# Memory keys of a decoder step: two column groups multiplied in turn, staggered first transfers, squares spread over later units

## The chip, the core and the metric

The kernel runs on one core of a Trainium2 chip, launched once. The metric is the device time of the launch in microseconds, the median of three runs. TensorE (PE) multiplies, ScalarE (ACT) and VectorE (DVE) work on rows of 128 partitions, GpSimd (POOL) and SyncE (SP) issue transfers, and every engine works through its own queue of instructions in the order in which they were placed there; semaphores hold an instruction until what it reads is there or what it overwrites has been read.

## The reference, cut to what matters

One layer of a decoder: an input projection, three branches (sliding-window attention, a state-space branch, attention into 256 memory tokens), a merge and a feed-forward block, for 256 prompt tokens and 8 samples. The change lies in the first part, which computes keys and values of the memory tokens:

```
def _rmsnorm(x, g):
    y = x * lax.rsqrt(jnp.mean(jnp.square(x), axis=-1, keepdims=True) + EPS)
    return y * g

def _mem_kv(mem, norm_mem, w_mem_kv, k_norm_mem):      # mem (256, 2048), w_mem_kv (2048, 2048)
    b, m, _ = mem.shape
    k, v = jnp.split(_rmsnorm(mem, norm_mem) @ w_mem_kv, 2, axis=-1)
    k = _rmsnorm(k.reshape(b, m, MEM_HEADS, MEM_HEAD_DIM), k_norm_mem)
    return k, v.reshape(b, m, MEM_HEADS, MEM_HEAD_DIM)
```

The rest follows on one core and is not touched; it reads the memory keys and values late.

## The kernel before, in words

**Units.** All weights are worked through as a list of units. A unit is a tile `raw` of 128x1024 fp32 (two blocks of 128 rows by 512 columns, 512 KB), loaded by SP (L261), split by ACT into a rounded part `hi` (L181) and by DVE into the remainder `lo` (L182), and multiplied on PE (L160). There are four `raw` buffers and three of `hi` and `lo`; `feed(i)` issues the load of unit i+4 and the split up to unit i+2 ahead of the products of unit i. A new `hi` waits until the last product of the unit three in front has read its buffer.

**Memory part.** Units 0 to 31. The product has 256 rows (two tiles of 128 memory tokens, `t`) and 2048 columns in four groups of 512: groups 0 and 1 are the keys, 2 and 3 the values. Each group is eight units, one after the other, and accumulates in two PSUM tiles `pmem` of 128x512. A unit gives 12 products of 128x512: two row blocks, two token tiles, and three terms each (`hi`x`memh`, `lo`x`memh`, `hi`x`meml`). `memh` and `meml` are the features: the rows of `mem_prompt`, loaded in pieces by `load_mem` (tiles `ring` for the first 128 tokens, `mem` for the second), transposed on PE (`memT`, L164) and split by ACT (`memh`, L348) and DVE (`meml`, L349) in `mem_feats`. The features of unit u+1 of group 0 are issued behind the first products of unit u.

**PSUM.** Two pools fill it: five tiles of 128x512 that the accumulators and the warm-up tile `idle` share, and three for short uses (`memT`, `kmT`, `rbx`, ...). A tile goes to a new user when the last reader of its old one is done.

**Norms.** `mem_norm` sums squares of the rows (eight ACT instructions of 128x512, `junk`, L360), then DVE forms `msv` and, by a shift and three Newton rounds (L171 to L176), `rs_m`. After the last unit of a key group `after_k` runs: four ACT sums `jk` (L404) that need `rs_m`, a chain of short DVE instructions, `km` (L413), its transposes `kmT` on PE and their copies on ACT. Values are scaled and stored by `after_v`. `prep_x` does for the rows of x what comes ahead of the input projection: sums of squares (`jkx`, L472), the inverse root, its spread `dgx`, `rbx`, then transposes `xT`.

**Order.** A scheduler sets each engine's queue from the order in the program, by its own estimates of time; `tc.issue_after(x)` holds what follows behind x. `mem_norm` and `prep_x` are generators that hand out a piece after each unit once they are ready (`rows` at unit 1, `go` at unit 9).

Of the kernel before, what the change touches and what calls it, by code (L numbers as in the profile page):

```python
# [23 lines left out]
KT = D // P  # L24
# [53 lines left out]
def tile_hybrid_decoder_step(  # L78
# [118 lines left out]

    def load_mem(f, n):

        for t in range(2):  # L200
            queue = nc.scalar if t and f < 2 else nc.sync
            h = f // 4
            if (t, h) not in mem_t:
                mem_t[t, h] = (lm if t else ld)("mem")
            c = slice(256 * (f % 4), 256 * (f % 4 + n))
            d = queue.dma_start(mem_t[t, h][:, c], mem_prompt[0, t * P:(t + 1) * P, h * 1024:(h + 1) * 1024][:, c])
            if f == 1:
                first["load1"] = d
# [48 lines left out]
    def load():  # L257
        n = state["dma"]
        raw = wp.tile([P, 1024], F32, tag="raw", name=nm("raw"), bufs=4)
        for j, (sl, src) in enumerate(units[n]["loads"](raw)):  # L260
            d = (nc.scalar if n == 0 and j else nc.sync).dma_start(sl, src)  # L261
        for f in behind.get(n, ()):
            with tc.issue_after(d.ins):
                f()
        raws[n] = raw
        state["dma"] += 1

    def feed(i):
        while state["dma"] < min(i + N_DMA + 1, len(units)):
            n = state["dma"]  # L270
            load()
            while state["split"] <= n - (N_DMA - N_SPLIT):
                do_split(state["split"])
        while state["split"] < min(i + N_SPLIT, len(units)):
            do_split(state["split"])

    def do_split(n):
# [12 lines left out]
        else:  # L290
            for k in range(2 if n == 0 else 1):
                c = slice(512 * k, 512 * k + 512) if n == 0 else slice(0, 1024)
                with tc.issue_after(state["memh", k if n == 0 else 1].ins):
                    state["split_at"], state["rest_at"] = split(hi[:, c], lo[:, c], raw[:, c])
# [57 lines left out]
    def mem_norm():  # L352
        junk = t2("junk", BF16)[:, 0:512]
        ssm_ = tiny("ssm", 8)
        for h in range(2):
            for t in range(2):
                for c in range(2):
                    o = 4 * t + 2 * h + c
                    with tc.issue_after(state["split_at"].ins):
                        act(junk, mem_t[t, h][:, c * 512:(c + 1) * 512], AF.Square, accum_out=ssm_[:, o:o + 1])  # L360
                    yield 0.6
        turn_vectors()
# [5 lines left out]
        yield 2  # L368

    def mem_group(cg):  # L370
        st = {}

        def prod(u):
            def f(hi, lo):
                if u == 0:
                    st["ps"] = [dps("pmem") for _ in range(2)]
                for n, (t, k) in enumerate(((0, 0), (1, 0), (0, 1), (1, 1))):
                    if cg == 0 and n == 1 and u < 7:

                        with tc.issue_after(m.ins):  # L380
                            mem_feats(u + 1)
# [4 lines left out]
                    mm(st["ps"][t], mh, wh, start=kk == 0, stop=False)  # L386
                    mm(st["ps"][t], mh, wl, start=False, stop=False)
                    m = mm(st["ps"][t], ml, wh, start=False, stop=kk == KT - 1)
# [36 lines left out]
        def loads(u):  # L425
            std = std_loads(w_mem_kv[0, 2 * u * P:(2 * u + 2) * P, cg * 512:(cg + 1) * 512])

            def f(raw):
                if cg == 0 and u in (1, 2, 4, 6):
                    load_mem(u, 1 if u == 1 else 2)  # L430
# [6 lines left out]
        for u in range(KT // 2):  # L437
            units.append(dict(
                loads=loads(u), 
                prod=prod(u), after=(after_k if cg < 2 else after_v) if u == KT // 2 - 1 else None))  # L440

    for cg in range(4):
        mem_group(cg)
# [1250 lines left out]
    side.add("m", mem_norm(), ["rows"])  # L1694
# [17 lines left out]
    load()  # L1712
    load()
# [5 lines left out]
    with tc.issue_after(state["turn"].ins):  # L1719
        warm_up(4)  # L1720
    for i, u in enumerate(units):
        feed(i)
        if i == 1:
            side.ready.add("rows")
        if i == 7:
            side.drain("m")
        if i == 9:
            side.ready.add("go")
# [45 lines left out]
```

## Time and profile before

| | |
|---|---|
| three runs | 1918.14, 1921.36, 1923.82 us; median 1921.36 |
| profiled execution | 1919.56 us, of which the span of the trace is 1917.8 us |
| PE busy | 1896.4 us, 99% of the span, 15359 matmuls |
| DVE, ACT, POOL busy | 1175.2, 961.2, 115.6 us |
| memory part | the first 90 us or so of the span |

The profile is of one execution on the one core. Times are counted from the start of the span. Busy time of a matmul runs to its modelled end, and matmuls overlap, so the distance from start to start tells what a product costs on the engine. A bracket behind a row tells how long the engine stood idle ahead of it and what ended that.

### The profile page before, as it was taken

What the parts mean: (1) busy time and instruction counts of PE and PEld (TensorE: products, weight loads), DVE (VectorE), ACT (ScalarE), POOL (GpSimd) and SP (SyncE); (2) the same over time, 40 slices, a digit from 0 to 9 for tenths busy, and PEclk for the clock granted to TensorE, in tenths of its full rate; (3) what the DMA queues carried; (4) which work ended last, traced back from release to release, by engine and by line L of the source; (5) the groups of instructions that cost most, each with busy time, mean ns of one, the idle gap of its engine ahead of it and who ended that gap; (6) DMA issues with size and microseconds to landing.
All of it is one profiled execution on the core that took longest, in us unless ns stands there. A gap on an engine that the chain in (4) does not pass through costs nothing.

```text
span 1917.8 us, 37599 instructions
## 1 busy us (share of the span) xinstructions
PE 1896.4 (99%) x15359; PEld 1849.4 (96%) x15359; DVE 1175.2 (61%) x2260; ACT 961.2 (50%) x1400; POOL 115.6 (6%) x238
## 2 busy tenths in 40 slices
PE   9999999999999999999999999999999999999998
PEld 7899999988998999999999999999999999999998
DVE  5755588655786977777455665555445555445554
ACT  6654466655677675565443544444334443334443
POOL 1110000010111111120000000000000000000000
PEclk9999999999999999999999999999999999999999
DMA  8776678677778878787666656665556665566663
GB/s 303 234 231 203 212 226 279 200 218 250 214 201 224 270 235 261 270 285 241 185 198 223 205 179 177 185 178 182 180 178 185 178 181 181 181 182 176 178 192 127
DMA packets 196497, 402.14 MB, mean 210 GB/s; under 512 B 16438, under 2 KB 21500, under 8 KB 196188
## 3 DMA queue, kind: packets, MB, share of 16 engines
q1 hardware_dynamic: 171568, 324.42, 55.7%
q0 software_dynamic: 19360, 69.14, 10.7%
q10 hardware_dynamic: 5396, 6.17, 0.9%
q8 instruction: 120, 1.97, 0.4%
q14 instruction: 53, 0.43, 0.1%
HBM read 375.74 MB, written 26.22 MB: 210 GB/s over the span
## 4 chain that ended last, share of the span: by engine, by line
PE 92%; DMA 4%; issue 1%; ACT 1%; DVE 1%; POOL 0%; SPq 0%; ACTq 0%; DVEq 0%; POOLq 0%
PE pin L160 31%; PE pu L160 13%; PE pdn L160 13%; PE pg L160 13%; PE pus L160 5%; PE pout L160 5%; PE pmem L160 4%; PE pua L160 1%; DMA ld<-in_cache_mem_v_dram 1%; PE pum L160 1%; DMA raw<-in_w_mem_kv_dram 1%; DMA out_dram<-rawT 1%; DMA raw<-in_w_up_swa_dram 1%; DMA raw<-in_w_in_dram 0%; PE py L160 0%
## 5 line engine op out<-in xcount | busy, mean ns | idle before, releaser
L182 DVE TENSOR_TENSOR lo<-raw,hi 128x1024 fp32r<-128x1024 f32 (+1 forms) x625 | 744.4, 1194 | 583.7 <-ACT hi L181 578.8
L181 ACT ACTIVATE hi<-raw 128x1024 fp32r<-128x1024 f32 (+1 forms) x625 | 645.4, 1036 | 853.6 <-PE pin L160 197.6
L160 PE MATMUL pin<-hl,hi 128*128 128x264 f32 x1728 | 491.0, 285 | 0.0
L160 PE MATMUL pin<-hh,hi 128*128 128x264 f32 x1728 | 490.5, 286 | 0.3 <-ACT hi L181 0.3
L160 PE MATMUL pin<-hh,lo 128*128 128x264 f32 x1728 | 485.6, 286 | 0.8 <-DVE lo L182 0.8
L160 PEld LDWEIGHTS pin<-hh,hi 128*128 128x128 f32 x1728 | 325.3, 189 | 3.8 <-issue 2.5
L160 PEld LDWEIGHTS pin<-hl,hi 128*128 128x128 f32 x1728 | 325.3, 188 | 3.8 <-issue 3.5
L160 PEld LDWEIGHTS pin<-hh,lo 128*128 128x128 f32 x1728 | 321.6, 188 | 3.8 <-issue 2.6
L160 PE MATMUL pdn<-fah,hi 128*128 128x264 f32 x704 | 199.7, 285 | 0.0
L160 PE MATMUL pdn<-fal,hi 128*128 128x264 f32 x704 | 199.4, 285 | 0.0
L160 PE MATMUL pu<-h2h,hi 128*128 128x264 f32 x704 | 199.3, 284 | 0.0
L160 PE MATMUL pu<-h2l,hi 128*128 128x264 f32 x704 | 199.3, 284 | 0.0
L160 PE MATMUL pg<-h2l,hi 128*128 128x264 f32 x704 | 199.1, 285 | 0.0
L160 PE MATMUL pg<-h2h,hi 128*128 128x264 f32 x704 | 198.4, 284 | 0.0
L160 PE MATMUL pdn<-fah,lo 128*128 128x264 f32 x704 | 197.0, 284 | 0.0
L160 PE MATMUL pu<-h2h,lo 128*128 128x264 f32 x704 | 196.6, 284 | 0.0
L160 PE MATMUL pg<-h2h,lo 128*128 128x264 f32 x704 | 196.1, 284 | 0.0
L160 PEld LDWEIGHTS pdn<-fah,hi 128*128 128x128 f32 x704 | 132.7, 189 | 0.1
L160 PEld LDWEIGHTS pu<-h2h,hi 128*128 128x128 f32 x704 | 132.7, 189 | 0.0
L160 PEld LDWEIGHTS pdn<-fal,hi 128*128 128x128 f32 x704 | 132.6, 188 | 0.1
L160 PEld LDWEIGHTS pg<-h2h,hi 128*128 128x128 f32 x704 | 132.6, 188 | 0.0
L160 PEld LDWEIGHTS pu<-h2l,hi 128*128 128x128 f32 x704 | 132.6, 188 | 0.0
(518 smaller groups left out, 2920.8 us busy)
## 6 DMA issues: line engine op xcount, KB each, us to landing
raw<-in_w_in_dram SPq DMA_DIRECT2D x216, 512.0 KB, 4.4
raw<-in_w_gate_dram SPq DMA_DIRECT2D x88, 512.0 KB, 3.7
raw<-in_w_up_dram SPq DMA_DIRECT2D x88, 512.0 KB, 4.1
raw<-in_w_down_dram SPq DMA_DIRECT2D x88, 512.0 KB, 4.2
raw<-in_w_up_ssd_dram SPq DMA_DIRECT2D x32, 512.0 KB, 4.1
raw<-in_w_out_dram SPq DMA_DIRECT2D x32, 512.0 KB, 4.3
raw<-in_w_mem_kv_dram SPq DMA_DIRECT2D x31, 512.0 KB, 3.8
ld<-in_cache_mem_v_dram POOLq DMA_DIRECT2D x16, 512.0 KB, 5.9
```

The source lines that it names most:

```text
L160: return nc.tensor.matmul(out, lhsT=lhsT, rhs=rhs, start=start, stop=stop)
L181: h = act(hi, src, AF.Copy)
L182: return h, V.tensor_tensor(lo, src, hi.bitcast(F32), op=ALU.subtract)
```

## The change

1. The list of units: key units of groups 0 and 1 alternate (00 10 01 11 02 12 03 13 04 14 05 06 15 07 16 17, group and unit), in four PSUM tiles; the values follow as before. Features of unit u are now issued behind the first products of the unit ahead of the one that reads them first.
2. `transfer()` keeps a list of what was sent; sendings 2 to 9 (counted from 0) each wait on SP until the third in front has landed (number 2 for number 0, the first piece of the rows). The second piece of the memory rows no longer goes over ACT's queue, and later pieces go behind a weight transfer.
3. Three loads instead of two stand ahead of the loop, the first splits are held back to three units, and the second warm-up has three matmuls in the program instead of four.
4. The eight squares are no longer handed out from unit 1 on but two at a time at units 4, 5, 9 and 12, `turn_vectors` comes at unit 4, and the rest of `mem_norm` (`msv`, `rs_m`) at unit 13.
5. `prep_x` may begin at unit 12 instead of 9.

SP's queue at the start, before (`ring` and `mem` are pieces of the memory rows, `raw` weights; the piece for the second token tile goes over ACT's queue for the first two sendings):

```order
L206 DMA ring<-in_mem_prompt_dram 128x256
L261 DMA raw_152<-in_w_mem_kv_dram 128x512
L206 DMA ring<-in_mem_prompt_dram 128x256
L261 DMA raw_155<-in_w_mem_kv_dram 128x2x512
L206 DMA ring<-in_mem_prompt_dram 128x512
L206 DMA mem_89<-in_mem_prompt_dram 128x512
L261 DMA raw_174<-in_w_mem_kv_dram 128x2x512
L261 DMA raw_188<-in_w_mem_kv_dram 128x2x512
```

And after, where the sendings from `raw_155` on each wait for one in front, as point 2 says:

```order
L218 DMA ring<-in_mem_prompt_dram 128x256
L274 DMA raw_152<-in_w_mem_kv_dram 128x512
L274 DMA raw_155<-in_w_mem_kv_dram 128x2x512
L218 DMA ring<-in_mem_prompt_dram 128x256
L218 DMA mem_89<-in_mem_prompt_dram 128x256
L274 DMA raw_157<-in_w_mem_kv_dram 128x2x512
L274 DMA raw_175<-in_w_mem_kv_dram 128x2x512
L218 DMA ring<-in_mem_prompt_dram 128x512
L218 DMA mem_89<-in_mem_prompt_dram 128x512
```

The second weight transfer has moved ahead of the second piece of the rows, and the wide pieces behind four weight transfers.

PE's queue at the turn from keys to values, before (`pmem_511` is the last key tile, `pmem_845` and `pmem_846` are the two tiles of the first value group):

```order
L160 MATMUL pmem_511<-hi_654,meml_116 128x512
L160 MATMUL pmem_845<-hi_693,memh_113 128x512
L160 MATMUL pmem_846<-hi_693,memh_113 128x512
L160 MATMUL pmem_845<-lo_694,memh_113 128x512
L160 MATMUL pmem_845<-hi_693,meml_115 128x512
L160 MATMUL pmem_846<-lo_694,memh_113 128x512
```

And after, from the end of the products for the first value tile (here `pmem_801`; the second is `pmem_802`); between the last key product and these rows stand 15 other products, all in `pmem_801`:

```order
L160 MATMUL pmem_801<-hi_714,memh_113 128x512
L160 MATMUL pmem_801<-lo_715,memh_113 128x512
L160 MATMUL pmem_801<-hi_714,meml_115 128x512
L160 MATMUL rbx_569<-dgx_566,ones 128x256
L164 MATMUL kmT_637<-ident,km_633 128x128 x4
L160 MATMUL pmem_802<-hi_578,memh_113 128x512
L160 MATMUL pmem_802<-lo_579,memh_113 128x512
```

The second value tile's products for three units (`hi_578` is the first of these) have moved behind the transposes of the first key tile.

DVE's queue at the same turn, before (from `rs_m` to the first instructions of the first `after_k`; this stood in the middle of the second key group):

```order
L367 COPY rs_m<-rs_y_366 128x2
L182 TENSOR_TENSOR lo_445<-raw_410,hi_444 128x1024
L182 TENSOR_TENSOR lo_507<-raw_440,hi_506 128x1024
L406 TENSOR_SCALAR ssk_460<-ssk_460 128x4
L171 TENSOR_SCALAR rs_y_467<-ssk_460 128x4
```

And after (`lo_579` belongs to the first value unit, `vx` is the sum over rows of x and `rs_y_553` its inverse root, `msv` the sum over memory rows):

```order
L182 TENSOR_TENSOR lo_579<-raw_504,hi_578 128x1024
L507 COPY vx_547<-xn_544 128x8
L506 TENSOR_TENSOR vx_547<-ssx_535 128x2
L510 TENSOR_SCALAR vx_547<-vx_547 128x10
L524 COPY xr_655<-xsT_550 128x4x8
L171 TENSOR_SCALAR rs_y_553<-vx_547 128x10
L172 TENSOR_SCALAR rs_y_553<-rs_y_553 128x10
L174 TENSOR_TENSOR rs_a_554<-rs_y_553 128x10
L381 TENSOR_REDUCE msv_582<-ssm_311 128x2
L175 SCALAR_TENSOR_TENSOR rs_a_554<-rs_a_554,vx_547 128x10
L182 TENSOR_TENSOR lo_678<-raw_574,hi_677 128x1024
```

`msv`, with which the way to `rs_m` begins, has moved behind `vx`, which reads the sums over all rows of x, and behind the first value unit's `lo`.

The diff:

```
@@ -195,17 +195,29 @@
     vb = t1("vb")[0:59, 0:P]
     vg = [t1("vg")[0:16, 0:P] for _ in range(2)]
 
+    sent = []
+
+    def transfer(ds):
+
+        if 2 <= len(sent) < 10:
+            for d in ds:
+                for e in sent[max(len(sent) - 3, 0)]:
+                    tc.add_manual_dep(d.ins, e.ins.name, mybir.DependencyInfo(
+                        mybir.DependencyClass.Sync, mybir.DependencyReason.DATA), reason="transfer")
+        sent.append(ds)
+
     def load_mem(f, n):
 
+        ds = []
         for t in range(2):
-            queue = nc.scalar if t and f < 2 else nc.sync
+            queue = nc.scalar if t and f == 0 else nc.sync
             h = f // 4
             if (t, h) not in mem_t:
                 mem_t[t, h] = (lm if t else ld)("mem")
             c = slice(256 * (f % 4), 256 * (f % 4 + n))
             d = queue.dma_start(mem_t[t, h][:, c], mem_prompt[0, t * P:(t + 1) * P, h * 1024:(h + 1) * 1024][:, c])
-            if f == 1:
-                first["load1"] = d
+            ds.append(d)
+        transfer(ds)
 
     nc.scalar.dma_start(vg[0], norm_mem[0].rearrange("(c p) -> c p", p=P))
     load_mem(0, 1)
@@ -257,8 +269,15 @@
     def load():
         n = state["dma"]
         raw = wp.tile([P, 1024], F32, tag="raw", name=nm("raw"), bufs=4)
+        ds = []
         for j, (sl, src) in enumerate(units[n]["loads"](raw)):
             d = (nc.scalar if n == 0 and j else nc.sync).dma_start(sl, src)
+            ds.append(d)
+            if n or not j:
+                state["raw"] = d
+        transfer(ds)
+        if n == 0:
+            first["load1"] = d
         for f in behind.get(n, ()):
             with tc.issue_after(d.ins):
                 f()
@@ -269,9 +288,9 @@
         while state["dma"] < min(i + N_DMA + 1, len(units)):
             n = state["dma"]
             load()
-            while state["split"] <= n - (N_DMA - N_SPLIT):
+            while state["split"] <= n - (N_DMA - N_SPLIT) and (i > 1 or state["split"] < N_SPLIT):
                 do_split(state["split"])
-        while state["split"] < min(i + N_SPLIT, len(units)):
+        while state["split"] < min(i + N_SPLIT if i > 1 else N_SPLIT, len(units)):
             do_split(state["split"])
 
     def do_split(n):
@@ -290,7 +309,7 @@
         else:
             for k in range(2 if n == 0 else 1):
                 c = slice(512 * k, 512 * k + 512) if n == 0 else slice(0, 1024)
-                with tc.issue_after(state["memh", k if n == 0 else 1].ins):
+                with tc.issue_after((state["memh", {0: k, 3: 3}.get(n, 1)] if n != 1 else state["split_at"]).ins):
                     state["split_at"], state["rest_at"] = split(hi[:, c], lo[:, c], raw[:, c])
         parts[n] = (hi, lo)
         state["split"] = n + 1
@@ -353,19 +372,17 @@
         junk = t2("junk", BF16)[:, 0:512]
         ssm_ = tiny("ssm", 8)
         for h in range(2):
-            for t in range(2):
-                for c in range(2):
+            for c in range(2):
+                for t in range(2):
                     o = 4 * t + 2 * h + c
-                    with tc.issue_after(state["split_at"].ins):
-                        act(junk, mem_t[t, h][:, c * 512:(c + 1) * 512], AF.Square, accum_out=ssm_[:, o:o + 1])
-                    yield 0.6
-        turn_vectors()
+                    act(junk, mem_t[t, h][:, c * 512:(c + 1) * 512], AF.Square, accum_out=ssm_[:, o:o + 1])
+                yield
         msv = tiny("msv", 2)
         V.tensor_reduce(msv, ssm_.rearrange("p (t c) -> p t c", t=2), axis=AX.X, op=ALU.add)
         V.tensor_scalar(msv, msv, 1.0 / D, EPS, op0=ALU.mult, op1=ALU.add)
         rs_m_ = rsqrt(msv, 2)
         V.tensor_copy(rs_m, rs_m_)
-        yield 2
+        yield
 
     def mem_group(cg):
         st = {}
@@ -375,17 +392,21 @@
                 if u == 0:
                     st["ps"] = [dps("pmem") for _ in range(2)]
                 for n, (t, k) in enumerate(((0, 0), (1, 0), (0, 1), (1, 1))):
-                    if cg == 0 and n == 1 and u < 7:
+                    if n == 1 and (cg, u) in turns:
 
                         with tc.issue_after(m.ins):
-                            mem_feats(u + 1)
+                            mem_feats(turns[cg, u])
                     kk = 2 * u + k
                     mh = memh(kk)[:, t * P:(t + 1) * P]
                     ml = meml(kk)[:, t * P:(t + 1) * P]
                     wh, wl = hi[:, k * 512:(k + 1) * 512], lo[:, k * 512:(k + 1) * 512]
-                    mm(st["ps"][t], mh, wh, start=kk == 0, stop=False)
+                    if (cg, u, n) == (1, 0, 0):
+                        with tc.issue_after(state["product"].ins):
+                            mm(st["ps"][t], mh, wh, start=True, stop=False)
+                    else:
+                        mm(st["ps"][t], mh, wh, start=kk == 0, stop=False)
                     mm(st["ps"][t], mh, wl, start=False, stop=False)
-                    m = mm(st["ps"][t], ml, wh, start=False, stop=kk == KT - 1)
+                    m = state["product"] = mm(st["ps"][t], ml, wh, start=False, stop=kk == KT - 1)
             return f
 
         def after_v():
@@ -426,21 +447,25 @@
             std = std_loads(w_mem_kv[0, 2 * u * P:(2 * u + 2) * P, cg * 512:(cg + 1) * 512])
 
             def f(raw):
-                if cg == 0 and u in (1, 2, 4, 6):
-                    load_mem(u, 1 if u == 1 else 2)
+                if cg == 0 and u in (1, 2, 4, 5):
+
+                    with tc.issue_after(state["raw"].ins):
+                        load_mem(u + u // 5, 1 if u == 1 else 2)
                 if cg == 0 and u == 0:
                     (d, src), = std(raw)
                     return [(d[:, k], src[:, k]) for k in range(2)]
                 return std(raw)
             return f
 
-        for u in range(KT // 2):
-            units.append(dict(
-                loads=loads(u), 
-                prod=prod(u), after=(after_k if cg < 2 else after_v) if u == KT // 2 - 1 else None))
-
-    for cg in range(4):
-        mem_group(cg)
+        return [dict(loads=loads(u), prod=prod(u), after=(after_k if cg < 2 else after_v) if u == KT // 2 - 1 else None)
+                for u in range(KT // 2)]
+
+
+    keys_order = [(int(c), int(u)) for c, u in "00 10 01 11 02 12 03 13 04 14 05 06 15 07 16 17".split()]
+    turns = {before: u for before, (c, u) in zip(keys_order, keys_order[1:]) if c == 0}
+    mem_units = [mem_group(cg) for cg in range(4)]
+    units += [mem_units[c][u] for c, u in keys_order]
+    units += mem_units[2] + mem_units[3]
 
 
     hh, hl = Feat("hh"), Feat("hl")
@@ -1691,7 +1716,7 @@
             down(i, base, 4 * ng, base == 8)
 
 
-    side.add("m", mem_norm(), ["rows"])
+    norm_steps = mem_norm()
     side.add("x", prep_x(), ["go"])
     side.add("c", consts())
     side.add("Mp", mem_prompt_work(), ["qm"])
@@ -1709,22 +1734,24 @@
         slow.add(f"Y{g}", ssd_sample_work(g), [f"y{g}"])
     slow.add("end", ssd_sample_end(), ["n3"])
     SIDE_US, SLOW_US = 1.0, 0.75
-    load()
-    load()
+    for _ in range(3):
+        load()
 
     with tc.issue_after(first["load1"].ins):
         h = act(warm[:, 0:1], warm[:, 0:1], AF.Copy)
     with tc.issue_after(h.ins):
         mem_feats(0)
     with tc.issue_after(state["turn"].ins):
-        warm_up(4)
+        warm_up(3)
     for i, u in enumerate(units):
         feed(i)
-        if i == 1:
-            side.ready.add("rows")
-        if i == 7:
-            side.drain("m")
-        if i == 9:
+        if i in (4, 5, 9, 12, 13):
+
+            with tc.issue_after(state["split_at"].ins), tc.issue_after(state["rest_at"].ins):
+                if i == 4:
+                    turn_vectors()
+                next(norm_steps)
+        if i == 12:
             side.ready.add("go")
         if i == 30:
             side.drain("x")
```

## Rows read from the trace of the kernel before

**Rows 1.** The page: span, and busy time of the engines.

```profile
span 1917.8 us, 37599 instructions
PE 1896.4 (99%) x15359; PEld 1849.4 (96%) x15359; DVE 1175.2 (61%) x2260; ACT 961.2 (50%) x1400; POOL 115.6 (6%) x238
```

**Rows 2.** Windows: length; PE, PEld, DVE, ACT, POOL busy; PEclk, DMA share, GB/s.

```profile
10.00:24.00 14.00, 12.90 (x61) 9.55 (x60) 8.65 (x12) 9.16 (x20) 0.57 (x1) 1.00 0.94 328
...
40.00:60.00 20.00, 20.00 (x93) 16.35 (x92) 14.40 (x40) 15.48 (x30) 1.64 (x3) 1.00 0.67 223
```

**Rows 3.** Timeline of PE, start and undisturbed products: start, us, engine, line, work, idle before.

```profile
4.18 0.69 PE L164 MATMUL memT<-ident,ring 128*128 128x128 f32 x2
6.33 0.69 PE L164 MATMUL memT<-ident,mem 128*128 128x128 f32 x2 [1.47 <-DMA mem<-in_mem_prompt_dram]
6.81 1.91 PE L160 MATMUL idle<-warm 128*128 128x128 f32 x8
8.38 1.14 PE L160 MATMUL pmem<-hi,memh 128*128 128x512 f32 x2
9.35 0.40 PE L160 MATMUL pmem<-lo,memh 128*128 128x512 f32 x1
...
24.12 0.39 PE L160 MATMUL pmem<-lo,memh 128*128 128x512 f32 x1
...
24.58 0.39 PE L160 MATMUL pmem<-lo,memh 128*128 128x512 f32 x1
```

**Rows 4.** Timeline of ACT, PEld and PE at stalls of the first units.

```profile
22.66 0.61 ACT L360 ACTIVATE junk<-mem 128x512 bf16<-128x512 f32 x1
...
23.27 0.82 ACT L348 ACTIVATE memh<-memT,vgc 128x256 fp32r<-128x256 f32 x2
...
16.94 0.19 PEld L160 LDWEIGHTS pmem<-hi,meml 128*128 128x128 f32 x1 [0.54 <-DVE meml L349]
...
23.78 0.50 PE L160 MATMUL pmem<-hi,memh 128*128 128x512 f32 x1 [0.86 <-ACT memh L348]
```

**Rows 5.** DMA issues of the page: count, KB each, median us to landing.

```profile
raw<-in_w_mem_kv_dram SPq DMA_DIRECT2D x31, 512.0 KB, 3.8
```

**Rows 6.** Timeline of ACT, sums of the first key group and of x.

```profile
41.94 0.48 ACT L404 ACTIVATE jk<-pmem,rs_m 128x256 f32<-128x256 f32 x1
...
42.54 0.47 ACT L404 ACTIVATE jk<-pmem,rs_m 128x256 f32<-128x256 f32 x1
...
49.93 1.06 ACT L472 ACTIVATE jkx<-x 128x1024 bf16<-128x1024 f32 x1
...
51.11 1.06 ACT L472 ACTIVATE jkx<-x 128x1024 bf16<-128x1024 f32 x1
...
52.17 1.04 ACT L181 ACTIVATE hi<-raw 128x1024 fp32r<-128x1024 f32 x1
```

**Rows 7.** Timeline of DVE, chain behind those sums, and a lo.

```profile
45.42 0.16 DVE L174 TENSOR_TENSOR rs_a<-rs_y 128x4 f32<-128x4 f32 x1
45.62 0.16 DVE L175 SCALAR_TENSOR_TENSOR rs_a<-rs_a,ssk 128x4 f32<-128x4 f32 x1
...
48.46 1.66 DVE L413 SCALAR_TENSOR_TENSOR km<-pmem,rs_y,knm_bc 128x256 f32<-128x256 f32 x4
...
57.94 1.22 DVE L182 TENSOR_TENSOR lo<-raw,hi 128x1024 fp32r<-128x1024 f32 x1
```

**Rows 8.** Timeline of PE, transposes and the spread of x's inverse root.

```profile
53.71 1.04 PE L164 MATMUL kmT<-ident,km 128*128 128x128 f32 x8
...
66.79 0.59 PE L160 MATMUL rbx<-dgx,ones 128*128 128x256 f32 x2
67.22 0.60 PE L164 MATMUL xT<-ident,x 128*128 128x128 f32 x4
```

**Rows 9.** PE's longest wait in the middle, and the window behind it.

```profile
801.03 0.60 PE L160 MATMUL pst<-Btok,xw 128*128 128x128 f32 x2 [4.13 <-DVE xw L1280]
...
801.00:805.00 4.00, 3.97 (x20) 4.00 (x21) 2.82 (x5) 2.67 (x6) 0.00 (x0) 0.57 0.49 166
```

## The prediction

> **What bounds the kernel now.** I read the page first: PE is busy 1896.4 of 1917.8 us [rows 1], so a change can only give what PE loses, and a gap put into PE's queue adds to the time in full, since nothing behind the memory part waits for anything else that long. PE's queue behind the memory part is the same row for row, so the sum is made over the first 90 us or so. Next the windows: from 10 to 24 us PE is busy 12.90 of 14.00 us with the DMA engines at 0.94, and from 40 to 60 us it has no idle time, ACT 15.48 and DVE 14.40 of 20 [rows 2]. Then the timeline of the start, the stalls, and last the chain behind the key sums, which the change moves to another place. A product of 128x512 costs 0.23 us from start to start (two from 24.12 to 24.58 [rows 3]), a unit of 12 thus 2.8 us.
>
> **The start: what it gives.** In the trace the first tile of rows is transposed at 4.18 us, the second only at 6.33, after 1.47 us of waiting for its transfer; eight warm-up matmuls follow, and the first product starts at 8.38 [rows 3]. The rows compete with all that SP sends at once. Now 768 KB (first weights and both pieces of rows) are under way until the rows have landed. The second tile should then land between 4.2 and 6.3; I take 5.2, gain 1.1. The warm-up's eight matmuls span 6.81 to 8.38, 0.2 each; two fewer give 0.4. But before 9.35 the products run at half speed: the first two take 0.97 together (8.38 to 9.35), twice the later spacing [rows 3]. If the speed still rises at about 9.35, products that start at 6.9 instead of 8.38 do half their work until then, and 1.5 us of earlier start is worth about 0.8; if it rises as much earlier, 1.5. I take 1.1. The Trainium skill ("TensorE: Matmul & The Clock Gate", part 1) says that the chip looks at activity in a window that runs freely and does not start with the kernel; by that the instant of the rise is nothing the change can place, and the sum would stand anywhere from 0.8 to 1.5.
>
> **The stalls up to 24 us.** PE loses 1.10 us of idle time there [rows 2]. Their cause is read in ACT's and DVE's queues: a square of 128x512 at 22.66 holds two `memh` until 23.27, and PE waits 0.86; `meml` costs another 0.54 at 16.94 [rows 4]. A product's row lasts 0.39 but the next starts 0.23 later [rows 3], so each of four breaks hides 0.16 more: 1.75 in all. Alternating key groups need a new pair of features in every second unit, 5.6 us instead of 2.8, and the squares lie later. So all of it can go; I take 1.8 of 0 to 1.9. With the start that is 2.9, in round numbers 3.0 (between 0.8 and 4.5, the last with the second tile of rows at 4.2 us and the speed risen with it).
> The price is the waits between transfers. A weight transfer lands 3.8 us after its issue in the median [rows 5]; with three under way one lands every 1.3 us against 2.8 us of products, so I cost them at nothing. The Trainium skill ("DMA: Bandwidth & Descriptors", "Anatomy of one DMA", written of GpSimd's transfers) puts about 2 us of each transfer down to completion rather than moving bytes; if each of the eight waits showed that 2 us to PE, it would be 16 us, but the landing time in the rows already holds it and three overlap.
>
> **The turn from keys to values: what it costs.** Here the change does most. Five PSUM tiles are shared by accumulators; one holds the warm-up, four now hold keys. The first value tile takes the warm-up's. The second must take a key tile, free only when `km` of the first key group has read it. PE works its queue in order: after the last key product it has 18 products for the first value tile (three units, all that the `hi` buffers hold), `rbx` and four `kmT`, and then the first product for the second tile. That is 18 x 0.23 = 4.14, plus 0.43 for `rbx` (66.79 to 67.22) and 0.5 for four `kmT` (eight last 1.04) [rows 8]: 5.1 us of work.
> When is `km` done? All times from the start of the last key product.
> - *ACT.* The `hi` of the last key unit waits for a product 41 rows in front, 9.0 us earlier. Behind it stand two squares, the short sum of the samples, a `memh`, four sums over x and a `hi`. With 0.40 until that product ends, 0.95 for each `hi`, 0.61 for a square, 0.41 for `memh` and as much for the short sum [rows 4, 6], and 1.18 for a sum (49.93 to 51.11 [rows 6]) that is 0.40 + 1.90 + 1.22 + 0.82 + 4.72 = 9.06: the last sum over x ends at about +0.1. The next `hi` ends at +1.4, the one after at +2.4.
> - *DVE.* `vx` waits for that sum; ten short instructions and the `lo` of 1.22 [rows 7] stand behind it, to +2.7. The next `lo` waits for its `hi`, to +4.2. Then 14 short instructions of two chains in turn, at 0.1 each since a dependent pair takes 0.20 (45.42 to 45.62 [rows 7]) and two chains fill it: +5.6. `dgx` and the copy 0.45, then four dependent ones at 0.20: `rs_m` at +6.9.
> - *ACT again.* Four `jk`, 0.60 each (41.94 to 42.54 [rows 6]): +9.3.
> - *DVE again.* 13 dependent short ones at 0.20, +11.9, and two `km` at 0.41 (four last 1.66 [rows 7]): +12.7; `kmT` of the second pair follow, +13.0.
> So the second value tile starts at +13.0 instead of +5.1: 7.9 us lost, 8.0 in round numbers, most of it in one unbroken wait ahead of `kmT`. The bounds: with `rs_m` ready at the last product 2.4 + 2.6 + 0.8 + 0.3 = 6.1 would remain, 1.0 lost; with the 14 short ones not overlapped (0.20 each), 9.4. I take the walk's 8.0, because each of its steps follows from the order of the queues. In the kernel before none of this touches PE: at 40 to 60 us it is busy throughout [rows 2], for the chain runs beside the second group, whose tiles are free.
> **The speed behind the wait.** PE's one long wait in the trace, 4.13 us before 801.03, is followed by a window with a granted clock of 0.57 over 4 us [rows 9]. At half speed for 3.4 of those 4 us it does 1.7 us less work. A wait of six us and more should cost the same, 1.7 (0 if the wait is cut in pieces).
> **The second turn.** The second tile of the second value group takes a tile of the second key group, whose `km` stands in DVE's queue behind a `lo` that ends 2.5 us after the last product of the group in front (0.40, 0.95 and 1.15) and behind 18 short instructions. At 0.11 to 0.2 each and 0.8 for `km` they end at 5.4 or later, against 18 products, 4.1 us: 1.2 lost or thereabouts (0 to 2.5).
>
> **Sum.** -3.0 + 8.0 + 1.7 + 1.2 = 7.9, say 8. The profiled execution becomes 1919.6 + 8 = 1927.6; the median of the runs lies 1.8 above that execution, so I forecast 1929.4 against 1921.36. About 0.3%, 5.8 us, is what a measurement of this kernel can tell from no change.
>
> **The rivals.**
> *The turn is covered (other side).* If `rs_m` and the sums are ready so early that the second value tile starts within 5.1 us of the last key product, nothing is lost there, and the start's 3.0 stand: 1918.4. What decides is ACT: if its four sums over x come some 8 us sooner than in my walk, because the features and squares of the last key units run ahead of PE. For it: ACT is free 4.5 of 20 us at 40 to 60 us [rows 2], and PE shows no wait at any turn there. Against it: the `hi` that stands ahead of the sums waits for PE itself, so ACT cannot run ahead of it; and in the queue 18 products of one value tile stand in front of the other, where before both take turns from the first product. 0.22.
> *The start starves.* If the staggered transfers land later than PE uses them, the stalls up to 24 us stay or grow. For it: the DMA engines are at 0.94 up to 24 us [rows 2], and a transfer that waits for a landing cannot start early, so one late landing moves all behind it. Then the start gains nothing and loses about 2: 8 + 3 + 2 = 13, 1934. Against it: the bytes per unit fall, since features are needed half as often. 0.10.
> *Half the wait.* If the x sums come 4 us sooner, or the queue's rows fill part of the wait, 3 to 4 us and the slow stretch remain: 4 + 1.7 - 3 = 2.7, about 1924. 0.08.
> The forecast itself keeps 0.60, its own range 1924 to 1934 (the loss at the turn from 5 to 9.4, the start from 0.8 to 4.5, the slow stretch or not).
>
> **How the numbers follow.** Slower by over 0.3% means above 1927.1: four fifths of the forecast's 0.60, and 0.09 of the starved start: 0.57. Faster means below 1915.6: only the covered turn with the upper end of the start's gain, 0.05. The rest is 0.38. The range 1918 to 1935 leaves out the lower half of the covered turn (0.11) and the upper ends of the forecast and of the starved start (0.08).
>
> **What would show it.** In the changed kernel's profile: the first product near 7 us instead of 8.4; no waits for `memh` or `meml` between 10 and 24 us; then, at 50 to 65 us, one long wait of PE ahead of `kmT` released by DVE's `km`, some six us, with `rs_m` on DVE behind `vx` and the `lo` rows, and the granted clock near half in the window behind it. I am wrong if the products of the second value tile begin within some 5 us of the last key product, or if PE waits for weights in the first 24 us.

## The result, and the profile after

Measured beside each other, the changed kernel took 1928.1 us and the kernel before 1920.1 us (medians of nine runs each): 8.0 us longer, ratio 1.0041 with a 95% interval of 1.0031 to 1.005. One of the changed kernel's nine runs took 4771.26 us; the ratio leaves it out, and without it the median would be 1927.97. The forecast was 1929.4 against 1921.36, so 8.0 us longer too. The profiled execution took 1928.52 us. Its page begins with the span and the busy times:

```profile
span 1926.8 us, 37591 instructions
PE 1900.8 (99%) x15357; PEld 1852.7 (96%) x15357; DVE 1175.3 (61%) x2260; ACT 962.1 (50%) x1400; POOL 114.8 (6%) x238
```

Against [rows 1] the span grew by 9.0 us and PE's busy time by 4.4; DVE and ACT do the same work. So PE waits more, and is longer at work on the same products. The windows of the changed kernel (columns as in [rows 2]) say where:

```profile
10.00:24.00 14.00, 13.81 (x63) 10.66 (x63) 7.70 (x9) 7.24 (x10) 0.00 (x0) 1.00 0.90 272
...
40.00:60.00 20.00, 19.08 (x87) 14.94 (x86) 10.45 (x20) 15.86 (x30) 1.06 (x2) 1.00 0.74 246
59.00:72.00 13.00, 6.20 (x26) 4.12 (x25) 9.61 (x51) 4.61 (x12) 0.00 (x0) 0.86 0.52 172
72.00:75.00 3.00, 3.00 (x10) 2.41 (x10) 0.55 (x2) 0.84 (x2) 1.09 (x2) 0.50 0.46 175
```

From 10 to 24 us the idle time fell from 1.10 to 0.19 us. From 40 to 60 us, where there was none, 0.92 has come. Between 59 and 72 us PE stands idle for 6.8 of 13 us, and in the three behind it runs at half clock (0.50). PE's timeline shows the two turns: the first, from the keys to the first value group, and the second, from there to the second value group. The wait stands in brackets:

```profile
64.80 0.67 PE L160 MATMUL rbx<-dgx,ones 128*128 128x256 f32 x2 [0.52 <-DVE rs_y L176]
71.43 1.11 PE L164 MATMUL kmT<-ident,km 128*128 128x128 f32 x4 [5.96 <-DVE km L434]
...
97.91 0.74 PE L164 MATMUL kmT<-ident,km 128*128 128x128 f32 x4 [0.48 <-DVE km L434]
```

The `kmT` at 71.43 answers to [rows 8], where it had no wait at all. The last key product starts at 59.10, the first product of the second value tile at 72.20: +13.1 us, where the prediction's walk through the queues had +13.0.

To see all losses on one scale I took the start of every PE instruction of the memory part and counted what exceeds 0.232 us for a product and 0.11 for a transpose. Both kernels have 384 products there. The two `rbx` are counted like transposes, so some 0.2 us of their own 0.43 us of work stand as a loss: before in products 210 to 287, in the changed kernel at the first turn. Times in us:

| stretch (products counted from 0) | before | after |
|---|---|---|
| first product starts | 8.38 | 6.98 |
| lost, products 0 to 23 | 0.80 | 2.17 |
| lost, 23 to 95 | 3.27 | 1.02 |
| lost, 95 to 143 | 0.08 | 1.78 |
| lost, 143 to 191 (last key product) | 0.25 | 0.24 |
| lost at the first turn, 191 to 210 | 0.03 | 8.08 |
| lost, 210 to 287 | 0.69 | 1.71 |
| lost at the second turn, 287 to 306 | 0.02 | 0.80 |
| the memory part ends | 110.78 | 118.79 |

Behind the memory part the changed kernel's trace is 0.95 us longer (1808.02 against 1807.07); eight transposes of x and six others that stood in it before come later there. So two premises of the prediction don't hold: the queue behind the memory part isn't the same row for row, and the part does not end at 90 us or so but at 110.78.

### The profile page after: what moved, and what is told of

It is laid out like the page before. It is cut to its first block, busy times and chain, and to the rows that moved or that the text cites. A ratio compares the mean times of both kernels' runs of the same rounds, so it can differ in the third digit from the quotient of the medians.

```text
span 1926.8 us, 37591 instructions
## 1 busy us (share of the span) xinstructions
PE 1900.8 (99%) x15357; PEld 1852.7 (96%) x15357; DVE 1175.3 (61%) x2260; ACT 962.1 (50%) x1400; POOL 114.8 (6%) x238
## 4 chain that ended last, share of the span: by engine, by line
PE 91%; DMA 5%; issue 1%; DVE 1%; ACT 1%; SPq 0%; POOL 0%; ACTq 0%; DVEq 0%; POOLq 0%
PE pin L160 31%; PE pu L160 13%; PE pdn L160 13%; PE pg L160 13%; PE pus L160 5%; PE pout L160 5%; PE pmem L160 2%; PE pua L160 2%; PE pum L160 2%; DMA raw<-in_w_mem_kv_dram 1%; DMA out_dram<-rawT 1%; DMA ld<-in_cache_mem_v_dram 1%; DMA mem<-in_mem_prompt_dram 1%; DMA raw<-in_w_in_dram 1%; PE py L160 1%
```

## The experiments

All were timed in five rounds beside the kernel before. "Lost" is counted as in the table.

**Is it the tile?** Six long PSUM tiles and two short ones instead of five and three:

```
-    pd = ctx.enter_context(tc.tile_pool(name="pd", bufs=5, space=PSUM))
-    pq = ctx.enter_context(tc.tile_pool(name="pq", bufs=3, space=PSUM))
+    pd = ctx.enter_context(tc.tile_pool(name="pd", bufs=6, space=PSUM))
+    pq = ctx.enter_context(tc.tile_pool(name="pq", bufs=2, space=PSUM))
```

> The changed kernel with six long and two short PSUM tiles instead of five and three. Theory (the wait is for a tile): the second value tile takes the sixth and needs no key tile, so PE alternates the two value tiles from the first product, the 6.2 us wait before kmT and the slow stretch behind it go, and the memory part ends at 109 to 110.5 us instead of 118.8. Whole time 1918 to 1920 if two short tiles are enough in the rest; longer if not, and then only the first 119 us tell. Rival (ACT and DVE are too late with hi and lo at this turn, whatever tile is free): PE waits some 5 us or more for hi or lo of the first value units, and the memory part still ends above 115 us.

Measured: 1926.62 us, ratio 1.0032 (1.002 to 1.0045). Windows of this kernel:

```profile
59.00:72.00 13.00, 13.00 (x57) 10.51 (x57) 9.67 (x39) 6.55 (x10) 0.00 (x0) 1.00 0.80 266
...
108.00:400.00 292.00, 289.44 (x2317) 280.01 (x2316) 192.62 (x470) 160.02 (x282) 22.50 (x43) 0.99 0.69 219
```

At the turn PE is busy for 13.00 of 13 us; 0.03 us are lost there instead of 8.08, and the memory part ends at 107.81 us, sooner than expected. The wait is for the tile. The whole time does not show it: from the first product of the input projection to the end it takes 1817.8 us, 9.8 more than in the changed kernel, with PE idle 2.6 us from 108 to 400 us (none in the changed kernel): work on x was pushed behind, and two short tiles are too few or the order they force is worse (these two were not told apart). The Trainium skill ("PSUM — Partial Sum Buffer", "Specifications (TRN2)") gives eight banks of 512 fp32 in a partition; five and three tiles of 128x512 use them all. This run takes its sixth long tile from the short ones; none tried six beside three.

**Is it the work on x that stands ahead?** Its start put back from unit 12 to 17:

```
-        if i == 12:
+        if i == 17:
             side.ready.add("go")
```

> The changed kernel, but the work on the rows of x may begin at unit 17 instead of 12, so its sums of squares stand behind the first key group's sums on ACT and DVE. Theory (the second value tile waits for km of the first key group, and rs_m is late because it stands behind the sums over x): rs_m then comes behind the third value unit's lo, at about +3.1 us after the last key product instead of +6.6, kmT of the first tile at about +9, PE's wait there shrinks from 8.1 us to 4.5, and the wait at the second turn goes (0.8 us): 1923.5 to 1925. Rival 1 (the sums over x are the whole cause): the wait shrinks to 1 us or less, 1919 to 1920. Rival 2 (they have no part in it): 1928 as it is.

Measured: 1925.48 us, ratio 1.0027 (1.0017 to 1.0037), a little above the expected 1923.5 to 1925. PE at the turn:

```profile
67.11 1.09 PE L164 MATMUL kmT<-ident,km 128*128 128x128 f32 x4 [4.55 <-DVE km L434]
```

5.42 us are lost instead of 8.08, 0.03 at the second turn instead of 0.80. The wait shrank to a size between the two rivals': the sums over x are a part of the cause and not the whole. The half speed behind this shorter wait lasted longer (granted clock 0.50 from 68 to 73 us), which the expectation did not count: products 210 to 287 lose 2.87 us here and 1.71 in the changed kernel.

**Is it the late norm?** Its last steps one to two units earlier, the work on x at unit 12 as in the change:

```
-        if i in (4, 5, 9, 12, 13):
+        if i in (4, 5, 9, 10, 11):
```

> The changed kernel with the last three pieces of the memory norm at units 9, 10 and 11 instead of 9, 12 and 13; the work on x still begins at unit 12. Theory now (the first key group's sums stand on ACT behind the copy of rbx, and so behind the whole chain of x, wherever rs_m is): rs_m is ready ahead of the last key product, but the four sums still start at about +7 us and kmT at about +12.5; the wait at the turn stays 7.5 to 8.5 us and the time 1927 to 1929. Rival (rs_m itself comes late because its squares and its chain were put back): the wait falls to 2 us or less, 1919.5 to 1921.5.

Measured: 1927.25 us, ratio 1.0042 (1.003 to 1.0054); 7.87 us lost at the turn. DVE, ACT and PE of this kernel, last key product at 59.73:

```profile
56.04 0.17 DVE L384 COPY rs_m<-rs_y 128x2 f32<-128x2 f32 x1
...
65.94 0.38 ACT L519 ACTIVATE rb<-rbx 128x256 f32<-128x256 f32 x1 [4.54 <-PE rbx L160]
66.22 0.47 ACT L425 ACTIVATE jk<-pmem,rs_m 128x256 f32<-128x256 f32 x1
...
71.87 1.09 PE L164 MATMUL kmT<-ident,km 128*128 128x128 f32 x4 [5.97 <-DVE km L434]
```

The copy into `rs_m` starts 3.7 us ahead of the last key product, and next to nothing is gained: the sums `jk` stand in ACT's queue behind the copy `rb`, which waits for `rbx` on PE and so for the whole chain of x. The changed kernel has two gates in a row, `rs_m` and `rb`, that open at about the same time.

**Both delays taken back**, that is the two edits above together:

> The changed kernel with both delays taken back and the key order and transfers left as they are: the memory norm's last pieces at units 9, 10, 11, and the work on x from unit 17 on. Theory (either delay alone holds the first key group's km; only both together free it): rs_m is ready ahead of the last key product, the four sums stand between two hi and end at about +2.6 us, km at about +5.8, so 1.5 to 2.2 us are lost at the turn instead of 8.1, and none at the second: 1919.5 to 1921.5. Rival (the place of the first group's last unit, one unit ahead of the end, matters as well): 3 us or more lost, 1922 or above.

Measured: 1921.06 us, ratio 1.0004 (0.9995 to 1.0014): no difference from the kernel before. 2.90 us are lost at the turn, more than the 1.5 to 2.2 expected:

```profile
65.78 0.83 PE L164 MATMUL kmT<-ident,km 128*128 128x128 f32 x4 [1.68 <-DVE km L434]
```

The first group's sums begin at 58.44, when its last product is done, and ACT's queue has a `hi` between each of the first three; the fourth ends at 62.4. That the first group ends only with the last products of the keys is thus worth another part, as the rival said, though it put 3 us or more; the kernel below that ends the group earlier, and has no waits between transfers, loses 1.57.

**Do the waits between transfers pay?** They are left out:

```
-        if 2 <= len(sent) < 10:
+        if 2 <= len(sent) < 2:
```

> The changed kernel without the waits of transfers for landings. Theory A (the staggering only moves a backlog: DMA engines idle up to 22 us, then full up to 43 us, where PE now waits 1.25 us): the waits at 43 to 45 us shrink to under 0.5, the second tile of rows lands at about 6.3 instead of 5.4 us, the first product starts about 0.9 us later, and the time stays within 1 us of 1928. Rival (the staggering keeps the first units fed): without it PE waits 2 us or more between 7 and 24 us, 1930 or above.

Measured: 1927.62 us, ratio 1.0039 (1.0027 to 1.0052). The second tile of rows is transposed at 5.77 us instead of 5.36, and PE has no idle time from 10 to 24 us:

```profile
5.77 0.44 PE L164 MATMUL memT<-ident,mem 128*128 128x128 f32 x2 [0.91 <-DMA mem<-in_mem_prompt_dram]
...
10.00:24.00 14.00, 14.00 (x67) 11.00 (x65) 8.63 (x10) 6.75 (x9) 0.00 (x0) 1.00 0.98 340
```

In the changed kernel the DMA engines moved 272 GB/s in that window; here it is 340. The first product starts at 7.18, only 0.20 later and not 0.9. Product 143 starts at 44.83 instead of 47.40, but not all of these 2.6 us are the waits' doing: in this execution PE was at full speed before its first product, and products 0 to 23 lose 0.86 instead of 2.17. Products 95 to 143 lose 0.33 instead of 1.78. The units are fed without the waits; the rival falls. The whole time shows 0.5 us of it, less than the runs can tell.

**The waits between transfers in the kernel before**, with nothing else of the change: the function `transfer` of the diff, called from `load_mem` and `load`.

> The kernel before with nothing but the waits of sendings 2 to 9 for a landing. Theory (staggering keeps the DMA engines from running ahead and gives the start little): the second tile of rows lands about 0.5 us earlier, PE then waits for weights or features between 10 and 45 us 1 to 2 us more; 1920 to 1922, no measurable change or slightly slower. Rival (the staggering is the useful part, and the alternation spoils it): 1917 or less.

Measured: 1921.72 us, ratio 1.0014 (1.0005 to 1.0022). PE at the start:

```profile
5.24 0.69 PE L164 MATMUL memT<-ident,mem 128*128 128x128 f32 x2 [0.38 <-DMA mem<-in_mem_prompt_dram]
7.27 2.08 PE L160 MATMUL idle<-warm 128*128 128x128 f32 x8 [1.35 <-ACT warm L1733]
```

The rows land 1.1 us earlier (5.24 against 6.33), but the first product starts at 9.00, for the warm-up waits for an ACT instruction that stands behind the sending of the second piece of the rows, and that sending now waits itself. Product 143 starts at 49.45 instead of 48.12. That is 0.62 us of later start and 1.17 more lost in products 0 to 23, most of it because in this execution PE was at half speed until after 12 us; products 23 to 143 lose 2.82 instead of 3.35. So alone the waits did not pay, at 1.8 us more in the median, but behind product 23 this profile shows no price for them.

**The keys in the old order**, one group after the other, with the rest of the start as in the change:

```
-    ... in "00 10 01 11 02 12 03 13 04 14 05 06 15 07 16 17".split()]
+    ... in "00 01 02 03 04 05 06 07 10 11 12 13 14 15 16 17".split()]
-        if i in (4, 5, 9, 12, 13):
+        if i in (3, 4, 5, 6, 7):
...
-                if i == 4:
+                if i == 3:
                     turn_vectors()
...
-        if i == 12:
+        if i == 9:
             side.ready.add("go")
```

> The changed kernel with the key units in the old order (group 0, then group 1), the squares at units 3 to 6, rs_m at 7, and the work on x from unit 9 on; the staggered transfers, three loads and short warm-up stay. Theory (alternation is what costs, the start gives little): km of the first group is done long before the values, no wait at either turn, 1919 to 1921, with the first product still near 7 us and waits for memh or meml of 1 to 3 us back between 10 and 37 us. Rival (the staggered start is worth its 3 us by itself): 1917 or less. Rival 2 (the start costs): 1923 or more.

Measured: 1920.72 us, ratio 1.0007 (0.9998 to 1.0016). The first turn loses 0.03 us as before, the second 0.35 (before 0.02). The waits for features are back:

```profile
12.53 0.74 PE L160 MATMUL pmem<-hi,memh 128*128 128x512 f32 x2 [0.63 <-ACT memh L367]
...
17.17 0.74 PE L160 MATMUL pmem<-hi,memh 128*128 128x512 f32 x2 [0.71 <-ACT memh L367]
```

Products 0 to 95 lose 6.5 us here, 3.2 in the changed kernel, 4.1 before, and 4.7 in the kernel before with the waits alone. So this start serves the old order worse than its own; whether by the waits or by where the rows stand in SP's queue was not told apart.

**Versions with a covered turn.** The first ends group 0 three units before the end of the keys, takes the norm at 9 to 11 and x from 17, and has no waits between transfers:

```
-    ... "00 10 01 11 02 12 03 13 04 14 05 06 15 07 16 17"
+    ... "00 10 01 11 02 12 03 13 04 14 05 06 07 15 16 17"
```

> The changed kernel with the first key group finished three units before the end of the keys (order ... 05 06 07 15 16 17), the norm's last pieces at units 9 to 11, the work on x from unit 17 on, and no waits between transfers. Theory: km of the first group then waits only for its own sums, which stand on ACT behind one hi that is free 2.8 us before the last key product, so kmT runs at about +5.5 to +6.5 against 4.6 us of work; 1 to 2 us lost instead of 8.1, no slow stretch behind it, no wait at the second turn: 1918 to 1920. Rival (something else at the turn holds PE, as hi and lo): 1923 or more.

Measured: 1918.56 us, ratio 0.9995 (0.9982 to 1.0007). 1.57 us are lost at the first turn, none at the second.

The next holds the `hi` of unit 16 behind the first group's sums; of two such kernels one lets x begin at unit 14, the other at 17:

```
-                with tc.issue_after((state["memh", {0: k, 3: 3}.get(n, 1)] if n != 1 ...
+                with tc.issue_after((state["jk", 0] if n == 16 else state["memh", {0: k, 3: 3}.get(n, 1)] if n != 1 ...
```

> As the kernel before this one, but the hi of unit 16 is issued behind the first key group's sums and the work on x begins at unit 14. Theory: the sums are done 5 us before the last key product and km by +4.5, so PE finds the second value tile free when it gets there: under 0.5 us lost at the first turn; the second key group's km stands behind the chain of x and costs 0.5 to 1.5 us at the second. The start's gain is then all that is left: 1917 to 1919, faster than the kernel before by 1 to 2 us at most. Rival: the alternation's start gives nothing in sum, and it is the same as before, 1919.5 to 1921.

Measured: 1922.66 us, ratio 1.0012 (1.0 to 1.0023). 0.77 us lost at the first turn, more than the 0.5 expected; the second turn now shows what the first showed in the change, the second group's `km` behind the chain of x:

```profile
87.70 0.74 PE L164 MATMUL kmT<-ident,km 128*128 128x128 f32 x4 [2.15 <-DVE km L435]
```

2.46 us are lost there. The memory part still ends at 108.58, 2.2 us before that of the kernel before; the trace behind it is 7.6 us longer (1814.7). Why is open: the order behind moved with the work on x, and this stretch differs among the other kernels with five and three tiles too (1805.9 to 1811.4 us in their profiles, one execution each).

> The version with the first key group finished three units early, norm at 9 to 11, x from unit 17 and no waits between transfers, and the hi of unit 16 behind the first key group's sums. Theory: the sums start 5 us or more ahead of the last key product, but km stands on DVE behind the lo of the third value unit, at about +5; 0.5 to 1 us lost at the first turn, none at the second: 1917 to 1919. Rival (order changes behind the memory part cost as in the kernel with x from unit 14): 1921 or above.

Measured: 1917.63 us, ratio 0.9983 (0.9974 to 0.9992): 2.4 us faster than the kernel before in the median, the only one of these whose interval stays below 1. That is less than the 0.3% the prediction asks of a difference. At the first turn 1.20 us are lost, of which the wait itself is small:

```profile
63.15 0.74 PE L164 MATMUL kmT<-ident,km 128*128 128x128 f32 x4 [0.36 <-DVE km L435]
```

## Why the prediction was right, point by point

**The start.** The second tile of rows is transposed at 5.36 (the step had 5.2), the first product starts at 6.98 (6.9). PE's timeline after, beside [rows 3]:

```profile
5.36 0.69 PE L164 MATMUL memT<-ident,mem 128*128 128x128 f32 x2 [0.49 <-DMA mem<-in_mem_prompt_dram]
5.84 1.49 PE L160 MATMUL idle<-warm 128*128 128x128 f32 x6
6.98 1.20 PE L160 MATMUL pmem<-hi,memh 128*128 128x512 f32 x2
...
9.69 0.92 PE L160 MATMUL pmem<-hi,memh 128*128 128x512 f32 x2
10.44 0.39 PE L160 MATMUL pmem<-lo,memh 128*128 128x512 f32 x1
...
12.19 0.50 PE L160 MATMUL pmem<-lo,memh 128*128 128x512 f32 x1 [0.19 <-DVE lo L182]
```

But up to the pair at 9.69 the products still come 0.43 us apart, so the rise to full speed came at about 10.3, 1.0 us later than before. 1.40 us of earlier start were given back as 1.37 more lost in products 0 to 23, about 1.1 of it at half speed and the rest around the wait for `lo` at 12.19: the 1.1 of the sum was in truth near nothing. That wait of 0.19 us is also a sign of being wrong that the prediction named, PE waiting for weights in the first 24 us, in small. A kernel with the same start and an early rise shows that the speed was not even the limit (at 10.80 PE waits for `hi`, and the last row, of ACT, shows `hi` waiting for its weights):

```profile
5.72 0.83 PE L160 MATMUL idle<-warm 128*128 128x128 f32 x6
6.86 0.74 PE L160 MATMUL pmem<-hi,memh 128*128 128x512 f32 x2 [0.30 <-ACT hi L181]
...
8.61 0.62 PE L160 MATMUL pmem<-hi,memh 128*128 128x512 f32 x2
9.07 0.40 PE L160 MATMUL pmem<-lo,memh 128*128 128x512 f32 x1
...
10.80 0.73 PE L160 MATMUL pmem<-hi,memh 128*128 128x512 f32 x2 [0.62 <-ACT hi L181]
```

```profile
9.69 1.06 ACT L181 ACTIVATE hi<-raw 128x1024 fp32r<-128x1024 f32 x1 [2.00 <-DMA raw<-in_w_mem_kv_dram]
```

This is the kernel with x from unit 17: full speed from 5.7 us on, yet product 23 starts at 14.71, in the changed kernel at 14.84. The weights set it, and with them the waits between transfers: in the two kernels without these waits that were at full speed before their first product, product 23 starts at 13.72 and 13.82.

**The stalls.** 1.8 us were taken; products 23 to 95 lose 2.25 less, but products 95 to 143 lose 1.70 more. From 23 to 143 the kernel before loses 3.35, the changed kernel 2.80, and the four alternating kernels without waits between transfers 1.33 to 1.35: the alternation does what the step said where nothing holds the transfers.

**The waits between transfers, costed at nothing.** This step failed. "Three under way, one every 1.3 us" forgot that SP is one queue: a sending that waits holds all behind it, the rows and x too. In the changed kernel the second unit's weights wait on SP for the first rows, and the second piece of the rows goes out behind them at 5.83 us; without the waits it goes out at 2.21:

```profile
1.27 4.51 SPq L274 DMA_DIRECT2D raw<-in_w_mem_kv_dram  x2
5.83 0.46 SPq L218 DMA_DIRECT2D ring<-in_mem_prompt_dram  x1
```

The median landing of [rows 5] does not show it: it is 5.0 us in the changed kernel and 4.9 without the waits. PE pays where the prediction did not look, at 40 to 45 us, ACT and PE:

```profile
40.29 1.06 ACT L181 ACTIVATE hi<-raw 128x1024 fp32r<-128x1024 f32 x1 [1.86 <-DMA raw<-in_w_mem_kv_dram]
42.89 1.06 ACT L181 ACTIVATE hi<-raw 128x1024 fp32r<-128x1024 f32 x1 [1.55 <-DMA raw<-in_w_mem_kv_dram]
...
44.01 0.74 PE L160 MATMUL pmem<-hi,memh 128*128 128x512 f32 x2 [0.68 <-ACT hi L181]
```

Over the runs: product 143 starts at 46.26 to 48.03 us in the five alternating kernels with these waits and at 44.83 to 46.52 in the four without, on the mean 47.3 and 45.6, so they cost about 1.7 us. From product 23 on, where all of them are at full speed, the five lose 1.78 to 3.16 up to product 143 and the four 1.33 to 1.35. The rival of the starved start was thus right in kind, though with less than its 5 us.

**The turn.** The size was right within 0.2 us (8.08 lost, or 7.9 with `rbx` charged its own work). ACT and DVE of the changed kernel, beside [rows 6, 7]; the last key product starts at 59.10:

```profile
57.80 1.06 ACT L497 ACTIVATE jkx<-x 128x1024 bf16<-128x1024 f32 x1
...
65.50 0.38 ACT L519 ACTIVATE rb<-rbx 128x256 f32<-128x256 f32 x1 [4.43 <-PE rbx L160]
65.78 0.47 ACT L425 ACTIVATE jk<-pmem,rs_m 128x256 f32<-128x256 f32 x1
```

```profile
58.99 0.16 DVE L506 TENSOR_TENSOR vx<-ssx 128x2 f32<-128x2 f32 x1 [0.33 <-ACT jkx L497]
...
60.16 1.23 DVE L182 TENSOR_TENSOR lo<-raw,hi 128x1024 fp32r<-128x1024 f32 x1
...
65.41 0.17 DVE L384 COPY rs_m<-rs_y 128x2 f32<-128x2 f32 x1
68.17 0.17 DVE L427 TENSOR_SCALAR ssk<-ssk 128x4 f32<-128x4 f32 x1 [2.58 <-ACT jk L425]
...
70.89 1.66 DVE L434 SCALAR_TENSOR_TENSOR km<-pmem,rs_y,knm_bc 128x256 f32<-128x256 f32 x4
```

The sums over x end at 58.9, `rs_m` at 65.6 (+6.5, the walk +6.9), the fourth `jk` at 68.1 (+9.0, walk +9.3), `km` begins at 70.9 (+11.8, walk +11.9). But the walk named one gate, `rs_m`, where there are two: `rb` ends at the same time, and the experiment with the early norm shows that it alone holds the sums as long. The 8 us are the later of two chains, not of one. So the prediction's lower bound was wrong: with `rs_m` ready at the last product it had 1.0 lost, and the run with the early norm lost 7.87.

**The speed behind the wait.** 1.7 was taken from [rows 9]. The granted clock is 0.50 from 72 to 75 us; the seven products from 72.20 to 75.26 take 3.06 us instead of 1.62: 1.4. The term is not tied to the wait's length: behind the 4.55 us of the kernel with x from unit 17 more was lost than behind these 5.96.

**The second turn.** 1.2 was taken, 0.8 is lost. The recorded sum slips a little: its 18 short instructions at 0.11 us put `km` at 5.3, not 5.4.

**The sum.** The start and the transfers together gave about 0.6 instead of 3.0 (1.40 - 1.37 + 2.25 - 1.70), the two terms behind the turn 1.8 by the table (1.02 and 0.78) instead of 2.9, and transposes worth 1.1 us left the memory part for later. So -0.6 + 8.05 + 1.8 - 1.1 and a rest of -0.2 make the 8.0 by which the memory part ends later. That the forecast came out at 8.0 as well is in part two errors that cancel: of its terms the turn alone had the right size, and the 8.0 to one decimal is luck.

## What to carry to other kernels

Count the buffers at the place where one group hands over to the next: a tile is free only when its last reader is done, and that reader's whole chain on the other engines stands on the path then. Follow every instruction that stands ahead of that reader in its queue, and look for a second gate behind the first; taking away one of two took next to nothing off the loss here, or a third. A wait put into the queue that issues transfers holds everything behind it, and its price may appear tens of microseconds later.

## What the runs showed of the hardware

PE's rise to full speed came at very different times in kernels whose first microseconds are alike: before 5.7 us in the kernel with x from unit 17 (row 5.72 above: six warm-up matmuls in 0.83 us), at about 11.2 in the last version, whose rows stand here:

```profile
6.61 1.49 PE L160 MATMUL idle<-warm 128*128 128x128 f32 x6
...
10.46 1.00 PE L160 MATMUL pmem<-hi,memh 128*128 128x512 f32 x2
11.30 0.39 PE L160 MATMUL pmem<-lo,memh 128*128 128x512 f32 x1
```

Both did the same ten warm-up matmuls from 1.53 us on. That the rise does not follow the kernel's start is what the Trainium skill says ("TensorE: Matmul & The Clock Gate", part 1), and these runs agree: between 5.7 and 11.2 us, and after 12 in the kernel before with the waits. One execution of each kernel was profiled, so a difference in the first 15 us between two profiles can be this and not the edit. The windows' column of the granted clock shows 1.00 there all the time; only the spacing of the products shows the half level.
